# Mixer projections with the high half of the weights meeting both halves of x in one 512-column matmul

## The chip, the cores and the metric

The kernel runs on one core of a Trainium2 chip. The metric is the device time of one launch in microseconds (us). Five engines work beside each other, each through its own queue in order: PE (TensorE, matrix products), ACT (ScalarE), DVE (VectorE), POOL (GpSimd) and SP (which issues transfers). PE writes to PSUM banks; ACT and DVE read them.

## The reference

An encoder trunk of two layers over 256 positions of width 1024, in float32. Each layer adds half a SwiGLU feed-forward block, a mixer, and another half feed-forward block:

```python
for l in range(DEPTH):
    x = x + FFN_RES * swiglu(rms_norm(x, ffn1_norm[l]), ffn1_w_gate[l], ffn1_w_up[l], ffn1_w_down[l])
    h = rms_norm(x, mix_norm[l])
    proj = h @ w_in[l]
    xr, gate, q, k, v = jnp.split(proj, SPLITS, axis=-1)
    y_rec = recurrent_group(xr, gate, conv_w[l], conv_b[l], lru_w_a[l], ...)
    y_att = windowed_gqa(q, k, v, attn_sink[l], rel_bias)
    y = jnp.concatenate([rms_norm(y_rec, lru_out_norm[l]), rms_norm(y_att, attn_out_norm[l])], axis=-1)
    x = x + y @ w_out[l]
    x = x + FFN_RES * swiglu(rms_norm(x, ffn2_norm[l]), ffn2_w_gate[l], ffn2_w_up[l], ffn2_w_down[l])
return rms_norm(x, final_norm)
```

In the mixer, `xr` goes through a convolution of four taps, two gates and a scan in each direction; `gate` goes through a GELU and multiplies the result of the scans; `q`, `k` and `v` feed attention with a window.

## The kernel before

Float32 products are made from split operands: every matrix is held as a high half, rounded to the fast float32 form, and a low half, the rest. A product is three matmuls: high by high, high by low, low by high. x is normed, transposed and split into one tile `xhl` that holds for each of 8 blocks of 128 rows its high half (256 columns, one per position) and its low half beside each other. Weights arrive as float32 (`raw`), are rounded by ACT (line 297; eight mixer halves by DVE, line 295) into `wh`, and DVE subtracts (line 298) to get `wl`. They go through a ring of eight slots and are prepared some pieces ahead of their use.

In the feed-forward stages `proj_pair` (lines 556 to 566) makes a tile of 128 outputs: per block one matmul of `wh` with both halves of x (512 columns) and one of `wl` with the high half (256 columns). The bank then holds two partial results, and `whole` (lines 741 to 746) adds them: ACT copies the second half of the bank to SBUF (line 744), DVE adds the first half to it (line 745).

In the mixer stage, `unit` (lines 827 to 831) makes a tile of 128 outputs with `proj` (lines 547 to 554): per block three matmuls of 256 columns, all into the same 256 columns of a bank, which hold the whole result. `unit` is called 12 times in each of the two layers: four times for the recurrence (`xr`, then `conv`, lines 860 to 876), four for its gate (`gelu`, lines 913 to 919) and four for the queries (`q`, lines 1089 to 1093, which splits the result into `q_t` on ACT and `ql_t` on DVE). All of them read the bank directly.

The order of the mixer's steps on PE is written out in `ORDER` (line 59) and is fixed, as are those of SP and POOL:

```python
ORDER = "x0 k0 x1 q0 l0 q1 l1 L0 x2 L1 x3 g0 l2 P0 q2 l3 V0 P1 s0 L2 g1 c0 c1 q3 V1 P2 L3 c2 y0 g2 y1 V2 P3 g3 c3 V3 D0 y2 y3 r0 O0 r1 O1 r2 r3 R0 R1 R2 R3 S0".split()
```

x, g and q are the three kinds of `unit`. l makes the gates of the recurrence from the convolved tile, c scans, y multiplies with the gate and splits, s takes a square root of all of it on ACT. L makes the logits of two heads from `q_t` and `ql_t`, P transposes the probabilities, V applies them to the values, D norms, O transposes the attention's result, r and R are the output product of the recurrent half. The order of ACT's and DVE's instructions is not written out in this stage: it is chosen when the program is built, by a planner with a cost model of its own. Banks of the pools `ps_c` and `ps_g` are handed out in turn (two of each), for the units, l and L; r and R take both banks of one of these pools.

Of the kernel before, what the change touches and what calls it, by code (L numbers as in the profile page):

```python
# [8 lines left out]
F32 = mybir.dt.float32  # L9
F32R = mybir.dt.float32r  # L10
AF = mybir.ActivationFunctionType
ALU = mybir.AluOpType
# [8 lines left out]
T = 256  # L21
# [46 lines left out]
def encoder_kernel(  # L68
# [31 lines left out]
    pe, act, dve, pool = nc.tensor, nc.scalar, nc.vector, nc.gpsimd  # L100

    def P(name, bufs, **kw):
        return ctx.enter_context(tc.tile_pool(name=name, bufs=bufs, **kw))
# [9 lines left out]
    sum_p = P("sum", 1)  # L113
# [11 lines left out]
    def bank(pool_):  # L125
        if pool_ == "gc":
            turn.append(turn.pop(0))
            pool_ = turn[0]
        return {"a": ps_a, "b": ps_b, "g": ps_g, "c": ps_c}[pool_].tile([128, 512], F32, tag=pool_, name="ps_" + pool_)
# [177 lines left out]
    def prefetch(target):  # L307
        while state["half"] <= min(target, state["cap"], len(halves) - 1):
            j = state["half"]
            n = turns.get(halves[j][0], 0)  # L310
            if n >= SLOTS and ring[n - SLOTS] not in used:
                return
            with ExitStack() as behind:
                for ins in state["behind"]:
                    behind.enter_context(tc.issue_after(ins.ins))
                prep_one()

    def W(*name):
        prefetch(index[name] + state["ahead"])
        return slot_t[name]  # L320

    def done(name):
        used.add(name)
        del slot_t[name]
# [222 lines left out]
    def proj(dst, w, t0, t1):  # L547
        wh, wl = w
        xh, xl = cur["h"], cur["l"]
        for k in range(KD):  # L550
            ks = slice(k * 128, (k + 1) * 128)
            pe.matmul(dst, wh[:, ks], xh[:, k, t0:t1], start=(k == 0), stop=False)  # L552
            pe.matmul(dst, wh[:, ks], xl[:, k, t0:t1], start=False, stop=False)
            pe.matmul(dst, wl[:, ks], xh[:, k, t0:t1], start=False, stop=(k == KD - 1))

    def proj_pair(dst, w):

        wh, wl = w
        x2 = cur["x"]
        for k in range(KD):  # L560
            ks = slice(k * 128, (k + 1) * 128)
            if k:
                pe.matmul(dst[:, 0:T], wl[:, ks], x2[:, 0, k, :], start=False, stop=False)  # L563
            pe.matmul(dst, wh[:, ks], x2[:, :, k, :], start=(k == 0), stop=(k == KD - 1))  # L564
            if not k:
                pe.matmul(dst[:, 0:T], wl[:, ks], x2[:, 0, k, :], start=False, stop=False)
# [248 lines left out]
    def mix(l):  # L815
        st = (l, 1)
# [6 lines left out]
        kl_t = mix_p.tile([128, T], F32R, tag="kl", name="kl_t")  # L823
        kv_t = mix_p.tile([128, 2, 256], F32, tag="kv", name="kv_t")
        late = {}

        def unit(name, i):
            ps = bank("gc")[:, 0:T]
            proj(ps, W(st, name, i), 0, T)
            done((st, name, i))  # L830
            return ps

        def head(t):
            if t == 0:
# [20 lines left out]
        def xr(i):  # L855
            ps = unit("xr", i)
            with tc.high_priority(offset=MIXF):
                conv(i, ps)
# [226 lines left out]
        def body():  # L1085
            def gate(i):
                gelu(i, unit("gt", i))

            def q(i):
                ps = unit("q", i)  # L1090
                act.activation(out=q_t[:, i, :], in_=ps, func=AF.Copy, scale=0.125)
                dve.scalar_tensor_tensor(out=ql_t[:, i, :], in0=ps, scalar=0.125, in1=q_t[:, i, :].bitcast(F32),
                                         op0=ALU.mult, op1=ALU.subtract)

            def den(_):
                att_den()
                att_norm(0)
                att_norm(1)

            def root(_):  # L1100
                act.activation(out=late["w"], in_=late["w"], func=AF.Sqrt)

            def stats(_):
                rec_stats()
                rec_evac(0)

            step = {"x": xr, "g": gate, "q": q, "l": lru_gate, "k": lambda _: head_end(), "s": root, "c": lru_scan,
                    "y": y_rec, "r": lambda k: rec(0, [k]), "R": lambda k: rec(1, [k]), "S": stats,
                    "L": att_logits, "P": att_pt, "V": att_pv, "D": den, "O": o_split, "f": lambda _: turn.reverse()}
            for n, i in ORDER:  # L1110
                step[n](int(i))
                if n == "D":
                    load_gain(3 * l + 2)
# [4 lines left out]
    with tc.manual_schedule(engines={engines.PE, engines.SP, engines.Pool}):  # L1118
        stages = [ffn((0, 0), None)]
        step = {"s": first_squares, "n": first_norm, "T": first_transposes, "m": stages[0][0]()}  # L1120
        for n, f in (("h", first_split), ("w", first_prep)):
            step[n] = lambda *a, f=f: f(False, *a)
            step[n.upper()] = lambda *a, f=f: f(True, *a)
        with tc.manual_schedule(engines={engines.Activation, engines.DVE}):
            setup_early()
            for _ in range(RAWS + 1):
                load_raw()
            for tok in FIRST:
                ins = step[tok[0]](*map(int, tok[1:]))
                if tok in BEHIND:  # L1130
                    state["behind"].append(ins)
        prefetch(3 + LEAD)
        state["behind"] = [ins]
        prefetch(3 + LEAD2)
        state["behind"] = []
        load_gain(1)
        for s in range(3 * DEPTH):
            _, body, tail, evac = stages[s]
            body()
            n = s + 1  # L1140
            if n == 3 * DEPTH:
                with tc.manual_schedule(engines={engines.Activation, engines.DVE}):
                    finish(tail, evac)
                break
            stages.append(mix(n // 3) if n % 3 == 1 else ffn((n // 3, n % 3), None))
            first = index[(n // 3, n % 3), "kv", 0] if n % 3 == 1 else index[(n // 3, n % 3), "g", 0]
            boundary(tail, evac, n, stages[n][0], first + (MAHEAD if n % 3 == 1 else 3))
# [46 lines left out]
```

## Time and profile before

| | |
|---|---|
| three runs | 951.38, 952.01, 953.37 us (median 952.01) |
| the profiled execution's own time | 952.4 us |
| its span | 950.6 us |
| PE busy | 927.3 us, 98% of the span |
| DVE busy | 705.0 us, 74% |
| ACT busy | 540.0 us, 57% |
| mean granted clock of PE | 0.992 of 2.4 GHz |

The span is the time from the first to the last instruction of the profiled execution. A share of busy time is an average over stages; which engine sets the pace in one stage has to be read from that stage. Matmuls are pipelined, so their durations overlap; the distance from one start to the next is what a matmul costs in a row of matmuls. The same is true to a smaller degree of DVE and ACT. Rows of a timeline have start and duration in us, engine, line of the kernel, operation, tile written and tiles read, count, and, in brackets, idle time before and what ended it.

### The profile page before, as it was taken

What the parts mean: (1) busy time and instruction counts of PE and PEld (TensorE: products, weight loads), DVE (VectorE), ACT (ScalarE), POOL (GpSimd) and SP (SyncE); (2) the same over time, 40 slices, a digit from 0 to 9 for tenths busy, and PEclk for the clock granted to TensorE, in tenths of its full rate; (3) what the DMA queues carried; (4) which work ended last, traced back from release to release, by engine and by line L of the source; (5) the groups of instructions that cost most, each with busy time, mean ns of one, the idle gap of its engine ahead of it and who ended that gap; (6) DMA issues with size and microseconds to landing.
All of it is one profiled execution on the core that took longest, in us unless ns stands there. A gap on an engine that the chain in (4) does not pass through costs nothing.

```text
span 950.6 us, 13902 instructions
## 1 busy us (share of the span) xinstructions
PE 927.3 (98%) x5407; PEld 811.6 (85%) x5407; DVE 705.0 (74%) x1192; ACT 540.0 (57%) x986; POOL 56.4 (6%) x66
## 2 busy tenths in 40 slices
PE   6799999999999999999999999999999999999997
PEld 6688888889989888888887888888999898888885
DVE  6967766768998866666589666666799887666663
ACT  7555555647864655555455555555587565555542
POOL 4400000000010000000070000000000100000000
PEclk9899999999999999999999999999999999999998
DMA  8865865625254856555646565556152566566521
GB/s 280 261 212 188 301 208 196 204 85 177 90 155 143 278 183 207 186 180 192 204 131 224 180 207 190 179 189 208 45 193 95 180 201 220 180 197 199 178 89 44
DMA packets 124994, 172.56 MB, mean 182 GB/s; under 512 B 3920, under 2 KB 108792, under 8 KB 124928
## 3 DMA queue, kind: packets, MB, share of 16 engines
q1 hardware_dynamic: 122192, 166.21, 54.3%
q0 software_dynamic: 2288, 4.87, 1.6%
q8 instruction: 42, 0.69, 0.3%
q10 hardware_dynamic: 448, 0.59, 0.2%
q14 instruction: 24, 0.20, 0.1%
HBM read 170.59 MB, written 3.16 MB: 183 GB/s over the span
## 4 chain that ended last, share of the span: by engine, by line
PE 91%; DVE 4%; ACT 2%; DMA 2%; issue 1%; POOL 0%; SPq 0%; POOLq 0%; DVEq 0%; ACTq 0%
PE ps_g L564 15%; PE ps_c L564 15%; PE ps_g L563 7%; PE ps_c L563 7%; PE ps_a L573 4%; PE ps_a L575 4%; PE ps_a L574 4%; PE ps_b L575 4%; PE ps_b L574 4%; PE ps_b L573 4%; PE ps_c L544 2%; PE ps_g L544 2%; DVE wl L298 1%; PE ps_a L997 1%; PE ps_g L552 1%
## 5 line engine op out<-in xcount | busy, mean ns | idle before, releaser
L298 DVE TENSOR_TENSOR wl<-raw,wh 128x1024 fp32r<-128x1024 f32 (+1 forms) x308 | 374.3, 1221 | 106.1 <-ACT wh L297 101.1
L297 ACT ACTIVATE wh<-raw 128x1024 fp32r<-128x1024 f32 (+1 forms) x294 | 300.3, 1032 | 87.3 <-PE ps_b L575 63.4
L564 PE MATMUL ps_g<-xhl,wh 128*128 128x512 f32 x640 | 233.7, 399 | 4.9 <-DVE hl L733 4.9
L564 PE MATMUL ps_c<-xhl,wh 128*128 128x512 f32 x640 | 232.6, 398 | 0.0
L563 PE MATMUL ps_g<-xhl,wl 128*128 128x256 f32 x560 | 157.3, 281 | 0.0
L563 PE MATMUL ps_c<-xhl,wl 128*128 128x256 f32 x560 | 156.7, 280 | 0.0
L564 PEld LDWEIGHTS ps_g<-xhl,wh 128*128 128x128 f32 x640 | 121.2, 189 | 28.5 <-issue 5.2
L564 PEld LDWEIGHTS ps_c<-xhl,wh 128*128 128x128 f32 x640 | 121.0, 189 | 23.1
L563 PEld LDWEIGHTS ps_g<-xhl,wl 128*128 128x128 f32 x560 | 106.6, 190 | 3.5
L563 PEld LDWEIGHTS ps_c<-xhl,wl 128*128 128x128 f32 x560 | 106.3, 190 | 3.5
L573 PE MATMUL ps_a<-wh,hh 128*128 128x512 f32 x168 | 65.8, 391 | 0.0
L573 PE MATMUL ps_b<-wh,hh 128*128 128x512 f32 x168 | 65.6, 391 | 0.0
L575 PE MATMUL ps_b<-wh,hl 128*128 128x512 f32 x168 | 65.4, 389 | 0.0
L575 PE MATMUL ps_a<-wh,hl 128*128 128x512 f32 x168 | 65.4, 389 | 0.0
L574 PE MATMUL ps_b<-wl,hh 128*128 128x512 f32 x168 | 65.4, 389 | 0.0
L574 PE MATMUL ps_a<-wl,hh 128*128 128x512 f32 x168 | 65.4, 389 | 0.0
L744 ACT ACTIVATE sg<-ps_g 128x256 f32<-128x256 f32 x40 | 15.4, 384 | 60.5 <-PE ps_g L564 60.2
L744 ACT ACTIVATE sg<-ps_c 128x256 f32<-128x256 f32 x40 | 15.4, 384 | 58.5 <-PE ps_c L564 58.4
L492 POOL TENSOR_TENSOR rstd<-rstd,half_t 128x1 f32<-128x1 f32 x16 | 11.2, 701 | 616.7 <-DVE rstd L489 488.2
L745 DVE TENSOR_TENSOR sg<-ps_g,sg 128x256 f32<-128x256 f32 x40 | 17.0, 425 | 31.8 <-ACT sg L744 31.8
L744 ACT ACTIVATE su<-ps_c 128x256 f32<-128x256 f32 x40 | 15.5, 386 | 40.8 <-PE ps_c L564 40.8
L744 ACT ACTIVATE su<-ps_g 128x256 f32<-128x256 f32 x40 | 15.4, 385 | 40.4 <-PE ps_g L564 40.4
(316 smaller groups left out, 1685.1 us busy)
## 6 DMA issues: line engine op xcount, KB each, us to landing
raw<-in_ffn_w_down_dram SPq DMA_DIRECT2D x44, 1024.0 KB, 5.0
raw<-in_ffn_w_gate_dram SPq DMA_DIRECT2D x43, 1024.0 KB, 5.4
raw<-in_ffn_w_up_dram SPq DMA_DIRECT2D x43, 1024.0 KB, 5.4
raw<-in_w_in_dram SPq DMA_DIRECT2D x14, 1024.0 KB, 5.4
raw<-in_w_out_dram SPq DMA_DIRECT2D x8, 1024.0 KB, 7.5
lb<-ld POOLq DMA_DIRECT2D x1, 2048.0 KB, 14.9
bias_t<-lb POOLq DMA_DIRECT2D x1, 1536.0 KB, 12.2
gain<-in_ffn_norm_dram SPq DMA_DIRECT2D x3, 512.0 KB, 4.4
```

The costliest lines, as they stand in the source:

```text
L297: act.activation(out=h3, in_=src, func=AF.Copy)
L298: dve.tensor_sub(out=l3, in0=src, in1=h3.bitcast(F32))
L492: pool.tensor_tensor(out=st[:, 1:2], in0=st[:, 0:1], in1=half_t, op=ALU.pow)
L544: pe.matmul(dst, (xh, xh, xl)[p][:, k, ts_], w[k // 4][p % 2][:, c], start=(p == 0 and k == 0), stop=(p == 2 and k == KD - 1))
L552: pe.matmul(dst, wh[:, ks], xh[:, k, t0:t1], start=(k == 0), stop=False)
L563: pe.matmul(dst[:, 0:T], wl[:, ks], x2[:, 0, k, :], start=False, stop=False)
L564: pe.matmul(dst, wh[:, ks], x2[:, :, k, :], start=(k == 0), stop=(k == KD - 1))
L573: pe.matmul(acc[hf], ah[:, ts_], wh[:, cs], start=first, stop=False)
L574: pe.matmul(acc[hf], ah[:, ts_], wl[:, cs], start=False, stop=False)
L575: pe.matmul(acc[hf], al[:, ts_], wh[:, cs], start=False, stop=last)
L744: act.activation(out=s, in_=ps[:, T:2 * T], func=AF.Copy)
L745: dve.tensor_tensor(out=s, in0=ps[:, 0:T], in1=s, op=ALU.add)
```

## The change

`unit` calls `proj_pair` in place of `proj`, takes a tile from the pool `sum_p` (its two buffers, `sg` and `su`, in turn), lets ACT copy the second half of the bank into it and DVE add the first half, and returns this SBUF tile. `conv`, `gelu` and `q` then read SBUF in place of the bank.

```diff
@@ -823,12 +823,17 @@
         late = {}
+        sums = ["sg", "su"]
 
         def unit(name, i):
-            ps = bank("gc")[:, 0:T]
-            proj(ps, W(st, name, i), 0, T)
+            ps = bank("gc")
+            proj_pair(ps, W(st, name, i))
             done((st, name, i))
-            return ps
+            sums.append(sums.pop(0))
+            s = sum_p.tile([128, T], F32, tag=sums[0], name="s")
+            act.activation(out=s, in_=ps[:, T:2 * T], func=AF.Copy)
+            dve.tensor_tensor(out=s, in0=ps[:, 0:T], in1=s, op=ALU.add)
+            return s
```

## Rows read from the trace of the kernel before

**Rows 1.** Page, part 1: busy time, share of the span, instructions of PE.

```profile
PE 927.3 (98%) x5407; PEld 811.6 (85%) x5407; DVE 705.0 (74%) x1192; ACT 540.0 (57%) x986; POOL 56.4 (6%) x66
```

**Rows 2.** Windows: us, busy of PE, PEld, DVE, ACT, POOL (instructions), PEclk, DMA, GB/s.

```profile
213.30:269.60 56.30, 56.24 (x484) 54.79 (x483) 52.25 (x125) 43.70 (x104) 0.00 (x0) 1.00 0.38 125
677.90:734.20 56.30, 56.26 (x484) 54.79 (x483) 52.25 (x125) 43.70 (x104) 0.00 (x0) 1.00 0.38 125
237.00:272.00 35.00, 35.00 (x297) 33.91 (x297) 34.79 (x84) 27.88 (x70) 0.59 (x1) 1.00 0.34 104
```

**Rows 3.** Timeline, PE: the first matmul of unit q0 and what follows the unit.

```profile
219.33 0.28 PE L552 MATMUL ps_c<-xhl,wh 128*128 128x256 f32 x1
...
222.21 0.28 PE L887 MATMUL ps_g<-xch,gh_t 128*128 128x256 f32 x1
```

**Rows 4.** Timeline, PE: two paired units of a feed-forward stage and what follows.

```profile
132.74 0.39 PE L564 MATMUL ps_c<-xhl,wh 128*128 128x512 f32 x1
...
135.56 0.40 PE L564 MATMUL ps_g<-xhl,wh 128*128 128x512 f32 x1
...
138.33 0.39 PE L573 MATMUL ps_a<-wh,hh 128*128 128x512 f32 x1
```

**Rows 5.** Timeline, feed-forward: copy on ACT, add on DVE, its reader, the next.

```profile
138.53 0.39 ACT L744 ACTIVATE su<-ps_g 128x256 f32<-128x256 f32 x1 [1.08 <-PE ps_g L564]
138.81 1.05 ACT L297 ACTIVATE wh<-raw 128x1024 fp32r<-128x1024 f32 x1
130.64 0.42 DVE L745 TENSOR_TENSOR su<-ps_g,su 128x256 f32<-128x256 f32 x1 [0.21 <-ACT su L744]
131.10 0.43 DVE L726 TENSOR_TENSOR th<-th,su 128x256 f32<-128x256 f32 x1
138.95 0.42 DVE L745 TENSOR_TENSOR su<-ps_g,su 128x256 f32<-128x256 f32 x1 [0.21 <-ACT su L744]
```

**Rows 6.** Lines 864 and 406: durations ns (min/median/max), first and last start.

```profile
L864 DVE TENSOR_SCALAR xc<-ps_g,par x6: 540/543/545, 216.4 to 702.1; 128x256 f32<-128x256 f32 x6
L406 DVE TENSOR_SCALAR xn<-x,rstd x8: 347/348/354, 7.0 to 13.7; 128x256 f32<-128x256 f32 x8
```

**Rows 7.** Line 552: what PE sat idle for before it (us, times).

```profile
  DVE xc L867: 0.5, 2
```

**Rows 8.** Timeline, ACT, DVE and PE: from q3 to the logits L3.

```profile
256.82 0.36 ACT L1091 ACTIVATE q_t<-ps_g 128x256 fp32r<-128x256 f32 x1
258.09 0.42 DVE L1092 SCALAR_TENSOR_TENSOR ql_t<-ps_g,q_t 128x256 fp32r<-128x256 f32 x1
258.38 0.28 PE L953 MATMUL ps_c<-kl_t,q_t 64*128 64x256 f32 x1
258.57 0.38 PE L954 MATMUL ps_c<-k_t,ql_t 64*128 64x256 f32 x1
```

**Rows 9.** Timeline, ACT, DVE and PE: from g3 to the product r3.

```profile
268.14 0.38 ACT L916 ACTIVATE x<-ps_g 128x256 f32<-128x256 f32 x1 [0.43 <-PE ps_g L554]
268.17 1.22 DVE L298 TENSOR_TENSOR wl<-raw,wh 128x1024 fp32r<-128x1024 f32 x1
269.31 0.42 DVE L917 SCALAR_TENSOR_TENSOR x<-x,ps_g 128x256 f32<-128x256 f32 x1
271.58 0.69 DVE L295 CAST wh<-raw 128x1024 fp32r<-128x1024 f32 x1
273.09 1.22 DVE L298 TENSOR_TENSOR wl<-raw,wh 128x1024 fp32r<-128x1024 f32 x1
274.22 0.48 DVE L933 SCALAR_TENSOR_TENSOR yl<-i_t,par,yh 128x256 fp32r<-128x256 f32 x1
275.23 0.39 PE L575 MATMUL ps_c<-wh,yl 128*128 128x512 f32 x1
```

**Rows 10.** Timeline, DVE and PE: the end of the mixer stage and the next stage's head.

```profile
286.19 1.21 DVE L298 TENSOR_TENSOR wl<-raw,wh 128x1024 fp32r<-128x1024 f32 x1
293.96 0.28 PE L544 MATMUL ps_c<-wh,xhl 128*128 128x256 f32 x1
```

## Prediction

> **What bounds the kernel now.** I read the page first: PE is busy 98% of the span [rows 1]. So a change pays if it shortens PE's work, as long as PE goes on without waits. The page's share is an average, so I then took the view of windows for the two stretches that the change touches, from the first projection unit of a mixer to the first output product. PE is busy in all but 0.06 us of the 56.3 us, at a granted clock of 1.00, which is the 2.4 GHz level. But DVE is busy for 52.25 us of the same 56.3 us, and ACT for 43.70; the second layer gives the same numbers [rows 2]. Away from the mixer DVE has room (74% over the span, [rows 1]); here it has 4.05 us. Most of this room lies at the start, where DVE has nothing to do until the first unit is done; from 237 to 272 us DVE is busy for 34.79 of 35 us, ACT for 27.88 [rows 2]. So the stage is bound by PE with DVE close behind it, and what has to be asked is whether the change makes DVE, or the chains through ACT and DVE, the bound.
>
> **What PE saves.** Before, a unit is 24 matmuls of 256 columns; q0 takes from 219.33 to 222.21, 2.88 us, which is 0.12 us for each [rows 3]. The paired form is in the trace already, in the feed-forward stages: 16 matmuls, 2.82 us for one and 2.77 us for the next [rows 4]. The saving is 2.88 - 2.82 = 0.06 to 2.88 - 2.77 = 0.11 us per unit; I take 0.08: of 155 such units in the feed-forward timeline 73 last 2.77 or 2.78 and 76 last 2.81 or 2.82. 12 units in a stage give 0.96 us (0.7 to 1.3).
>
> There is a second gain. The bank of a unit is now held until the last of its readers; for the convolution that is DVE's fourth instruction, line 867, and PE waits for it twice, once per layer, for 0.5 us together [rows 7]. After the change the bank is free after the add. So 0.25 us more per stage, if the copy and the add are not late themselves. Together 1.2 us per stage, 2.4 us in all.
>
> [...]
>
> **What ACT and DVE get.** 12 copies and 12 adds per stage. In the feed-forward stages the copy holds ACT for 0.28 us (138.53 to 138.81) and the add follows its start after 0.42 us (138.53 to 138.95); the add's result is used by the next DVE instruction 0.46 us after the add's start (130.64 to 131.10) [rows 5]. So
>
> - ACT has 12 x 0.28 = 3.4 us more, on 43.70 of 56.3.
> - DVE has 12 adds more. The add lasts 0.42 us; with the overlap that ACT shows between neighbours (0.39 us long, 0.28 apart) I count 0.34 of it, as between other neighbours on a busy DVE: 4.1 us. Against this the first step of the convolution, which reads the bank in 0.543 us, will read SBUF; the nearest row for that is the same operation on an SBUF tile, 0.348 us [rows 6]. 4 x 0.195 = 0.8 us less. Net 3.3 us per stage (between 2.5, if other readers gain also, and 5.0, if the adds count in full).
> - Each chain from a unit to its consumer gets 0.42 + 0.46 = 0.88 us longer, if both engines are free at once, and more if the add has to queue.
>
> So DVE's load becomes 52.25 + 3.3 = 55.55 us in a stretch that is to shrink from 56.3 to 55.1. This doesn't fit, unless work leaves the stretch. What can leave it: weight preparation for the tail of the stage. DVE makes two such weights (a rounding, line 295, and a subtraction, line 298; the second at 271.58 and 273.09, the subtraction of the first at 268.17) ahead of the split that r3 needs [rows 9]; each costs 0.6 + 1.2 = 1.8 us, and both are used after r3. Behind r3 DVE's last weight of the stage is done at 287.4, 6.5 us ahead of the next stage's head at 293.96 [rows 10]. So 3.6 us can be put off without harm, if the planner does put them off. No transfer is added or moved; the loads of the next weights start when a raw tile is free, and a preparation put off by 3 us delays them by as much, inside these 6.5 us.
>
> The new copy makes ACT wait for the unit, and for the reader of two units before, since there are two sum buffers. Units are at least 2.9 us apart; behind a copy that waits there stand weight roundings, tanhs and exps, and behind these DVE. I cost this at nothing; if a reader of the convolution is late by more than this distance, it costs what it is late.
>
> **Where PE will wait.** Two places have no room for 0.88 us:
>
> - L3. The split of q3 is late now: ACT comes to it at 256.82, after the exps of the second-last heads, DVE at 258.09 to 258.51, and PE's third logits matmul, normally 0.12 us behind the second, starts 0.19 us behind it, at 258.57 [rows 8]. After the change PE comes to this place earlier by 10 units x 0.08 + 0.25 = 1.05 us, and `ql_t` comes later by up to 0.88 us. So the wait is 1.05 to 1.93 us: everything that was gained so far is lost, whatever its size, and up to 0.88 us more. Least is lost if the copy goes ahead of the exps. I take 1.5.
> - r3. The chain from g3 ends with the split at 274.22 to 274.70, and its matmul starts at 275.23, room of 0.53 us [rows 9]. It gets 0.88 us longer: a wait of 0.35 us. It is 0 if the weight pair goes behind the chain, and about 3 us if the whole load of DVE arrives here. I take 0.25, as the planner had already put these pairs later than others of their kind.
>
> **Sum.** Per stage -1.2 + 1.5 + 0.25 = +0.55 us, for two stages +1.1 us. From the profiled execution (952.4 us, span 950.6) that is 953.5; the median of the runs is 0.4 us lower, so 953.1 us.
>
> **Rivals.**
> 1. All is hidden: the planner places copies and adds well, L3 and r3 don't wait. For it: at most places chains have some 2 us of room, banks come free earlier, and 3.6 us of DVE's work can move. Against it: no room at L3 [rows 8]. 952.0 - 2.4 = 949.6 us.
> 2. DVE becomes the bound, and the time is longer. Mechanism: the planner goes by its own costs and leaves the weight pairs where they are; then 3.3 us of adds and 0.9 us of the first chain's delay, less the 0.53 us of room and some 0.4 of small gaps, end at r3, as PE comes there: 3.3 + 0.9 - 0.53 - 0.4, about +3.3 us per stage against now, less what is put off after all; with one rounding of 0.6 us put off, +2.7. It decides the sign from the point where DVE puts off less than about 2.3 us: then +1.0 per stage is left, over 0.2% in all. For it: DVE's 55.55 in 55.1 us [rows 2]. Against it: the slack behind r3 [rows 10]. 952.0 + 2 x 2.7 = 957.4 us.
> 3. The pairing saves less in the mixer than in the feed-forward stages. At 0.06 us per unit rival 1 gives 952.0 - 1.9 = 950.1; the forecast doesn't move, because there the late split sets the time and not PE. [...]
>
> **Chances.** A difference of 0.2% (1.9 us) is about what a measurement of this kernel can tell from no change. Rival 1 has 0.15 (with rival 3 inside it, some of it within 0.2%), rival 2 has 0.25, the forecast 0.60; its own range is from 951 (L3 waits for only what PE gained) to 955 (both places pay in full, 2 x (0.88 + 0.35 + some queueing)), so a quarter of it is slower by over 0.2%. Faster 0.14, same 0.46, slower 0.40. The range goes from 950.0, which leaves out the lower part of rival 1, to 957.5, which takes in most of rival 2.
>
> **What the profile will show.** Units of 2.77 to 2.82 us with 16 matmuls; line 864 at 0.35 us; no idle time of PE before g0; DVE at over 95% of the stretch; a gap of more than 0.2 us ahead of PE's line 954 in L3, and one ahead of r3; line 295 and 298 pairs behind 274 us. I am wrong if L3 starts a microsecond earlier than now (the copy went ahead), or if DVE's pairs stay and PE waits for 3 us at r3.

## The result and the profile after

The changed kernel takes 964.13 us (median of four runs, 961.04 to 964.44) against 952.27 us of the kernel before on the same chip: a ratio of 1.0118, 95% interval 1.0106 to 1.0130. The forecast was 953.1 us with a range to 957.5. The change costs some 12 us, ten times the 1.1 us that the sum gave.

The page after, part 1, answers [rows 1]:

```profile
PE 931.9 (97%) x5215; PEld 805.3 (84%) x5215; DVE 711.6 (74%) x1216; ACT 547.6 (57%) x1010; POOL 54.3 (6%) x66
```

DVE got 6.6 us more (711.6 against 705.0), ACT 7.6 us (547.6 against 540.0): 3.3 and 3.8 us a stage, where the sum had 3.3 and 3.4. PE has 192 matmuls less, and yet 4.6 us more of busy time. So the work added was sized well, and the loss is elsewhere.

The view of windows for the same two stretches, from the first unit of the mixer of the first layer on, against [rows 2]:

```profile
211.85:268.15 56.30, 52.07 (x337) 45.45 (x335) 50.47 (x125) 43.79 (x106) 0.00 (x0) 0.94 0.35 115
237.00:272.00 35.00, 32.08 (x213) 28.74 (x212) 33.62 (x82) 27.50 (x69) 0.00 (x0) 0.90 0.31 96
```

PE is busy in 52.07 of 56.3 us, where it was in 56.24: 4.2 us of idle time came in. Its clock is 0.94 in place of 1.00. DVE is busier in neither window (50.47 against 52.25 us, 33.62 against 34.79): the stage now gets less far in the same time.

PE's waits, over the whole span (us in total, times, longest), the lines that are new against before:

```profile
PE ps_c L957 <- ACT q_t L1096: 2.9, 2, 1.5
...
PE ps_g L893 <- DVE xcl L881: 2.3, 3, 1.0
PE ps_c L959 <- DVE ql_t L1097: 1.8, 2, 0.9
...
PE ps_c L893 <- DVE xcl L881: 1.0, 2, 0.6
PE ps_g L892 <- ACT xch L880: 0.4, 1, 0.4
```

Lines 957 and 959 are the logits (L3 in the order), lines 892 and 893 the gates of the recurrence (l0 to l2); `xch` and `xcl` are the halves of the convolved tile's split. The waits come to 8.4 us. None of them is at r3: from 262 to 296 us no row of PE shows idle time.

The next table follows PE through both mixer stages: each step's start against the same step before, both counted from the stage's first matmul, as the PE timelines of the two traces have them. The stage grew from 80.60 to 87.32 us, the second from 80.59 to 87.16. Together that is 13.3 us; the first stage begins 1.5 us earlier than before (211.85 against 213.36), in work that the change doesn't touch.

| up to the start of | us later than before, stage 1 | stage 2 | what lies between |
|---|---|---|---|
| l0 | -0.19 | -0.22 | three units, each 0.04 to 0.11 shorter |
| L0 | +1.61 | +0.30 | waits for `xcl` in l0 (stage 1 alone) and l1 |
| g0 | +1.07 | -0.23 | two units; the bank wait of [rows 7] is gone |
| P0 | +1.68 | +1.51 | wait for `xcl` in l2, in stage 2 for `xch` as well |
| P2 | +1.67 | +1.49 | |
| L3 | +3.20 | +3.03 | wait for `q_t` |
| g2 | +4.85 | +4.66 | L3: wait for `ql_t`, then slower matmuls |
| V2 | +6.79 | +6.62 | the unit g2 itself, at half the clock |
| end | +6.72 | +6.57 | nothing more |

So a stage loses some 1.6 us up to P2, after what the units save, and some 5 us between P2 and V2; the sum had 0.55 us in all.

**Around L3.** The timeline of after, on ACT, DVE and PE, against [rows 8]:

```profile
257.25 0.19 ACT L971 ACTIVATION_READ_ACCUMULATOR pr<-pr,stn 128x1 f32 x1
257.34 0.36 ACT L834 ACTIVATE s<-ps_c 128x256 f32<-128x256 f32 x1
257.61 0.36 ACT L834 ACTIVATE s<-ps_g 128x256 f32<-128x256 f32 x1
257.98 1.09 ACT L990 ACTIVATE pt<-ps_b 128x512 f32<-128x512 f32 x2
259.06 0.42 ACT L921 ACTIVATE x<-s 128x256 f32<-128x256 f32 x1
259.39 0.42 ACT L1096 ACTIVATE q_t<-s 128x256 fp32r<-128x256 f32 x1
...
257.69 0.66 DVE L912 SCALAR_TENSOR_TENSOR i_t<-i_t,w_t 128x512 f32<-128x512 f32 x1
258.28 0.41 DVE L932 TENSOR_TENSOR i_t<-i_t 128x256 f32<-128x256 f32 x1
258.61 0.41 DVE L835 TENSOR_TENSOR s<-ps_c,s 128x256 f32<-128x256 f32 x1
258.95 0.41 DVE L835 TENSOR_TENSOR s<-ps_g,s 128x256 f32<-128x256 f32 x1
259.28 0.67 DVE L914 TENSOR_TENSOR_SCAN i_t<-a_t,i_t 128x256 f32<-128x256 f32 x1
259.88 0.66 DVE L916 TENSOR_TENSOR_SCAN i_t<-a_t,i_t 128x256 f32<-128x256 f32 x1
260.46 0.39 DVE L922 SCALAR_TENSOR_TENSOR x<-x,s 128x256 f32<-128x256 f32 x1
260.77 0.41 DVE L1097 SCALAR_TENSOR_TENSOR ql_t<-s,q_t 128x256 fp32r<-128x256 f32 x1
...
259.85 0.38 PE L957 MATMUL ps_c<-k_t,q_t 64*128 64x256 f32 x1 [1.47 <-ACT q_t L1096]
261.24 0.58 PE L959 MATMUL ps_c<-k_t,ql_t 64*128 64x256 f32 x1 [0.89 <-DVE ql_t L1097]
```

Before, the last exp ended at 256.65:

```profile
256.46 0.19 ACT L966 ACTIVATION_READ_ACCUMULATOR pr<-pr,stn 128x1 f32 x1
```

ACT then split q3 straight from the bank, behind one step of the GELU (256.82), and DVE followed at 258.09. Now q3 goes ACT, DVE, ACT, DVE, and it queues at each step. ACT copies it at 257.61; DVE, which has no idle time here, adds it at 258.95, behind a step of the scans (line 912), one of y0 (line 932) and the add of g1; only then can ACT make `q_t` (259.39); DVE makes `ql_t` at 260.77, behind two scans and a step of the GELU. From the last exp's end (257.44 now, 256.65 before) to the logits' third matmul are 3.8 us in place of 1.9: 1.9 us longer, where the working had at most 0.88. The exps themselves end 2.3 us later in the stage than before, 0.6 us more than PE's own delay at P2; the waits at L3 are made of both.

**Behind L3.** Windows of 1 us; the figure behind POOL's bracket is the granted clock:

```profile
258.00:259.00 1.00, 0.38 (x4) 0.15 (x2) 1.00 (x4) 1.00 (x2) 0.00 (x0) 1.00 0.00 0
259.00:260.00 1.00, 0.15 (x1) 0.15 (x2) 1.00 (x4) 0.80 (x3) 0.00 (x0) 1.00 0.00 0
260.00:261.00 1.00, 0.35 (x2) 0.15 (x2) 1.00 (x3) 0.12 (x1) 0.00 (x0) 0.73 0.00 0
261.00:262.00 1.00, 0.76 (x6) 0.76 (x8) 1.00 (x4) 0.30 (x1) 0.00 (x0) 0.50 0.00 0
...
266.00:267.00 1.00, 1.00 (x4) 0.81 (x4) 1.00 (x4) 0.20 (x2) 0.00 (x0) 0.50 0.00 0
267.00:268.00 1.00, 1.00 (x8) 0.93 (x7) 0.20 (x1) 0.06 (x1) 0.00 (x0) 0.85 0.41 90
268.00:269.00 1.00, 1.00 (x11) 1.00 (x11) 0.65 (x2) 1.00 (x3) 0.00 (x0) 1.00 1.06 279
```

PE is idle for most of 258 to 261 us; then its clock is 0.50, the 1.2 GHz level, up to 267. The unit g2 takes from 262.82 to 267.74, 4.92 us, where it took 2.98 before (259.48 to 262.46). The first matmul of g2 and of V2 behind it, before and after:

```profile
259.48 0.39 PE L552 MATMUL ps_c<-xhl,wh 128*128 128x256 f32 x1
262.46 1.90 PE L997 MATMUL ps_a<-kv_t,pt 128*128 128x64 f32 x16
...
262.82 0.79 PE L564 MATMUL ps_c<-xhl,wh 128*128 128x512 f32 x1
267.74 1.89 PE L1002 MATMUL ps_a<-kv_t,pt 128*128 128x64 f32 x16
```

The matmuls of L3, from line 959's first to g2, take 1.58 us (261.24 to 262.82) in place of 0.91 (258.57 to 259.48). So the clock costs 1.94 + 0.67 = 2.6 us a stage, and the waits ahead of it 1.5 + 0.9 = 2.4. The Trainium skill ("TensorE: Matmul & The Clock Gate", section "Part 1: The HAM clock gate") says that an idle TensorE falls back to the lower of two clock levels. The rows agree on the level, 0.50; PE had not been wholly idle before it, but busy for 0.88 of the 3 us.

**At l0.** Timeline of DVE and PE, after:

```profile
219.12 0.69 DVE L295 CAST wh<-raw 128x1024 fp32r<-128x1024 f32 x1 [1.21 <-DMA raw<-in_w_in_dram]
219.85 1.23 DVE L298 TENSOR_TENSOR wl<-raw,wh 128x1024 fp32r<-128x1024 f32 x1
...
220.99 0.42 DVE L881 TENSOR_TENSOR xcl<-xc,xch 128x256 fp32r<-128x256 f32 x1
...
221.46 0.39 PE L893 MATMUL ps_g<-xcl,gh_t 128*128 128x256 f32 x1 [0.67 <-DVE xcl L881]
```

`xch` was ready at 218.36. But DVE had by then gone to a weight whose data hadn't landed, waited 1.21 us for it, and made both halves of it before the split that PE needed. Here DVE is not short of time: the split stands in the wrong place of its queue. In the second stage DVE's order is the same, but the weight had landed (DVE rounds it at 689.07, right behind the convolution), and PE doesn't wait at l0. So the loss at l0 also hangs on when a transfer lands. Before, only the rounding stood ahead of the split, and the subtraction behind it; `xcl` was done at 220.41 and PE read it at 222.33, right behind the start of l0 in [rows 3]:

```profile
219.99 0.42 DVE L876 TENSOR_TENSOR xcl<-xc,xch 128x256 fp32r<-128x256 f32 x1
```

That is 1.9 us of room.

### The profile page after: what moved, and what is told of

It reads as the page before. It is cut to its first block, busy times and chain, and to the rows that moved or that the text cites. A ratio compares the mean times of both kernels' runs of the same rounds, so it can differ in the third digit from the quotient of the medians.

```text
span 962.3 us, 13552 instructions
## 1 busy us (share of the span) xinstructions
PE 931.9 (97%) x5215; PEld 805.3 (84%) x5215; DVE 711.6 (74%) x1216; ACT 547.6 (57%) x1010; POOL 54.3 (6%) x66
## 4 chain that ended last, share of the span: by engine, by line
PE 82%; DVE 10%; DMA 3%; issue 2%; ACT 2%; POOL 0%; POOLq 0%; ACTq 0%; DVEq 0%
PE ps_g L564 16%; PE ps_c L564 16%; PE ps_g L563 7%; PE ps_c L563 7%; PE ps_a L573 4%; PE ps_a L575 4%; PE ps_a L574 4%; PE ps_b L575 4%; PE ps_b L573 4%; PE ps_b L574 4%; DVE wl L298 3%; PE ps_c L544 2%; PE ps_g L544 1%; DMA raw<-in_w_in_dram 1%; PE ps_g L566 1%
## 5 line engine op out<-in xcount | busy, mean ns | idle before, releaser
L564 PE MATMUL ps_g<-xhl,wh 128*128 128x512 f32 x752 | 274.1, 399 | 4.5 <-DVE hl L733 4.5
L564 PE MATMUL ps_c<-xhl,wh 128*128 128x512 f32 x720 | 265.4, 402 | 0.0
L563 PE MATMUL ps_g<-xhl,wl 128*128 128x256 f32 x658 | 184.3, 280 | 0.0
L563 PE MATMUL ps_c<-xhl,wl 128*128 128x256 f32 x630 | 177.7, 282 | 0.0
L564 PEld LDWEIGHTS ps_g<-xhl,wh 128*128 128x128 f32 x752 | 141.9, 189 | 32.0 <-issue 4.8
L564 PEld LDWEIGHTS ps_c<-xhl,wh 128*128 128x128 f32 x720 | 137.7, 191 | 27.2 <-PE ps_g L958 0.4
L563 PEld LDWEIGHTS ps_g<-xhl,wl 128*128 128x128 f32 x658 | 124.8, 190 | 4.1
L563 PEld LDWEIGHTS ps_c<-xhl,wl 128*128 128x128 f32 x630 | 121.3, 192 | 4.1
L492 POOL TENSOR_TENSOR rstd<-rstd,half_t 128x1 f32<-128x1 f32 x16 | 9.2, 577 | 629.6 <-DVE rstd L489 487.4
L732 ACT ACTIVATE hh<-th 128x256 fp32r<-128x256 f32 x80 | 33.4, 417 | 8.5 <-DVE th L726 8.2
```

What stands on the lines that cost most here:

```text
L732: act.activation(out=hh, in_=src, func=AF.Copy)
```

## The experiments

Two theories went into them. "Chains": the copy and the add lengthen the way from a unit to its reader, the reader is late at l0 to l2 and L3, and the clock falls behind L3. "Load": DVE is simply full, and each added operation counts alike, wherever it stands. A third was that paired matmuls are slower here. In every version the planner chose the order on ACT and DVE anew, so a run can differ in other places than the edited one.

### One half of the change alone

e1_pair_only calls `proj_pair` and returns the first half of the bank; e2_sum_only keeps the old matmuls and does the copy and a second pass over the bank:

```diff
 e1, against after:
             proj_pair(ps, W(st, name, i))
             done((st, name, i))
-            sums.append(sums.pop(0))
-            s = sum_p.tile([128, T], F32, tag=sums[0], name="s")
-            act.activation(out=s, in_=ps[:, T:2 * T], func=AF.Copy)
-            dve.tensor_tensor(out=s, in0=ps[:, 0:T], in1=s, op=ALU.add)
-            return s
+            return ps[:, 0:T]
 e2, against before:
             proj(ps, W(st, name, i), 0, T)
             done((st, name, i))
-            return ps
+            sums.append(sums.pop(0))
+            s = sum_p.tile([128, T], F32, tag=sums[0], name="s")
+            act.activation(out=s, in_=ps, func=AF.Copy)
+            dve.tensor_tensor(out=s, in0=ps, in1=s, op=ALU.max)
+            return s
```

> The change's matmuls without its copy and add: conv, gelu and q read the first 256 columns of the bank, so the product of the high half of the weights with the low half of x is left out of the 24 units. Theory 'chains' (the time comes from the copy and the add in the way of l0, l1, l2 and L3): PE keeps its saving, 952.3 - 2.4 = 950 us, from 949 to 951. Rival 'the paired matmuls are slower in the mixer': clearly above 953 us, towards 964. Theory 'load' (DVE is simply full) gives 950 too.

> The three 256-column matmuls of before, with a copy on ACT and an operation of the add's size on DVE behind each unit (a maximum of the bank and its copy, which gives the same values). Theory 'chains': the waits are set by ACT and DVE, not by PE, so nearly the whole loss is here without the change's matmuls: 963 to 966 us. Rival 'paired matmuls': about 952 to 954. Theory 'load': like 'chains'.

Measured: e1 952.7 us, ratio 1.0008 [0.9999, 1.0018]; e2 961.69 us, ratio 1.0095 [1.0074, 1.0117]. The loss is in the copy and the add: e2 alone has four fifths of it, with the waits at the same places, though less than the 963 us and more that were expected. That paired matmuls are slower is out: e1 has them and none of the loss. That e1 isn't faster was a miss. Its units are shorter by 0.07 us each, as costed, but the stages are 80.63 and 81.24 us long against 80.60 and 80.59. PE's waits in e1 show where that went:

```profile
PE ps_c L564 <- DVE xc L868: 1.6, 2, 1.2
PE ps_g L564 <- ACT i_t L897: 0.4, 2, 0.2
```

PE arrives earlier at banks that the convolution (line 868) or the gates' reader (line 897) still hold, and waits there. In this order of the steps PE's gain was not to be had, even without the copy and the add; e12 below has it in another order.

### One kind of unit at a time

Each of these uses the new form for one name only, and the old form for the others (`if name not in (...)` ahead of the new lines):

> The change for the four query units of each layer alone; the others as before. Theory 'chains': the wait at L3 (3.2 us per stage in the trace of the changed kernel) and the fall of the clock behind it (1.9) are both here, the waits at l0, l1, l2 (0.8 to 0.9 each) are not: 2 x 5.1 less 8 x 0.08, 961 to 962 us. Theory 'load' (each added operation counts alike, a third of 12 us): 956 us.

> The change for the four recurrence units of each layer alone. Theory 'chains': the waits at l0, l1 and l2 for the split of the convolved tile are here (0.8 to 0.9 us each per stage in the changed kernel), the wait at L3 isn't: 2 x (2.6 less 0.35 of bank wait and 0.3 of matmuls), 956 us. Theory 'load': a third of 12 us, 956 us too; the stretches of the trace tell them apart: under 'chains' PE's loss stands at l0 to l2, nothing at L3.

> The change for the four gate units of each layer alone: the same number of added operations as for q or x, but their result is needed late (y), so no tight chain gets longer. Theory 'chains': 952 us, between 951 and 953.5. Theory 'load': a third of 12 us like each other kind, 956 us.

Measured: queries 959.68 us, ratio 1.0076 [1.0054, 1.0099]; recurrence 956.68, 1.0041 [1.0023, 1.0059]; gate 954.06, 1.0024 [1.0015, 1.0034]. Four copies and four adds a stage cost 2 us or 7, depending on who reads the result. The queries' figure lies between the two theories (956 and 961 to 962). With the queries alone there are the waits at L3 and the clock's fall (the unit g2 +2.06 and +1.15 us in the two stages). With the recurrence alone the expected cost was at l0 to l2; it turned out to be smaller there (0.7 us between l0 and L0, of which 0.1 is left at P0) and larger at L3 (+1.35), where DVE made `ql_t` 0.7 us late and the GELU of g1 held the bank of g2 for 0.5 us; in the second stage the clock fell behind it (g2 +1.51 us). So the delay turns up at another place than the lengthened chain, and the pure "chains" reading was too narrow. With the gate alone the small loss is spread over L3 and the end of the stage, between both expectations (952 and 956).

### The clock behind L3

e4_fill keeps the change and gives PE twelve matmuls of 512 columns, whose results no one reads, ahead of L3:

```diff
+            if i == 3:
+                for n in range(12):
+                    pe.matmul(banks[n % 2], cur["h"][:, n % KD, 0:128], cur["x"][:, :, n % KD, :], start=True, stop=True)
```

> The changed kernel with 12 matmuls of 512 columns more per layer (2.8 us at 2.4 GHz) ahead of the logits L3, into banks that L3 then overwrites. If the fall of the clock to 1.2 GHz behind L3 comes from PE's wait there, PE now works through the 1.5 us and most of the 0.9 us in which it waited, keeps 2.4 GHz, and g2 takes 2.9 us in place of 4.9: 964 less 2 x 2 us or some more, 959 to 961 us, although PE has 5.6 us more to do. If the clock falls for another reason, the time is the same or longer: 964 to 967 us.

Measured: 958.17 us, ratio 1.0062 [1.0047, 1.0077], a little under the 959 to 961 us expected. With some 5.5 us more of PE work (24 matmuls 0.23 us apart), the kernel is some 6 us shorter than after. Two windows of it:

```profile
260.00:261.00 1.00, 1.00 (x13) 0.97 (x12) 1.00 (x4) 0.28 (x1) 0.00 (x0) 1.00 0.00 0
261.00:262.00 1.00, 1.00 (x7) 0.79 (x6) 1.00 (x3) 0.51 (x1) 0.00 (x0) 1.00 0.00 0
```

The clock stays at 1.00, and g2 is 0.09 us shorter than before in the first stage, in place of 1.94 longer. From P2 to V2 the stage is 2.4 us longer than before, some 2.7 us of it the fillers, where after is 5.1 us longer: the fillers fill the waits, and the 2.7 us a stage that are won are about the clock's fall. The waits at l0 to l2 are smaller too (+0.50 and +0.40 at P0, where after has +1.68 and +1.51), so some 2.3 us of the gain come from there. This shows the clock's part of the loss; as the fillers cover the waits as well, it doesn't size it to the tenth.

### More room for the chains

e7_l3_later puts g2 ahead of L3, g3 ahead of P3 and r0 ahead of V3; e9_both_later also q1 ahead of l0, x2 ahead of l1, and so on. e10 and e11 are the kernel before with the same orders, e12 is e1 with both shifts:

```diff
 e7:
-... q3 V1 P2 L3 c2 y0 g2 y1 V2 P3 g3 c3 V3 D0 y2 y3 r0 O0 ...
+... q3 V1 P2 g2 L3 c2 y0 y1 V2 g3 P3 c3 r0 V3 D0 y2 y3 r1 O0 ...
 e9, besides:
-x0 k0 x1 q0 l0 q1 l1 L0 x2 L1 x3 ...
+x0 k0 x1 q0 q1 l0 x2 l1 L0 x3 L1 ...
```

> The changed kernel with the unit g2 ahead of L3 in the order of PE's steps (and g3 ahead of P3, r0 ahead of V3, so that the steps behind L3 have cover as well); the same work. Theory 'chains': the split of q3 has 2.8 us more, the wait at L3 (3.2 us) and the low clock behind it (1.9) go, while l0 to l2 still wait: 964 - 10 and up to 1 us of new waits per stage, 954 to 956 us. Theory 'load': DVE's work is the same, so PE waits elsewhere: 962 us or more.

> The changed kernel with two shifts in the order of PE: L3 one or two steps later as in e7 (there 4.1 us over before were left), and now also l0 behind q1 in place of ahead of it, l1 behind x2, L0 and L1 one step later each. Chains: what e7 had left is mostly the waits ahead of l0, l1 and l2; they go too, 953 to 955 us. Load: VectorE has as much to do, and the waits turn up at other steps behind it; no change against e7, 956 to 957 us.

> The kernel before with only the shift of e7 in its order (L3, P3 and V3 later). A control: if the shift itself costs something (a wait ahead of O0, where e7 had 1.2 us), it is 953 to 955; if the shift is free, 951.5 to 952.5; both theories say at least 951.

> The kernel before with both shifts of e9. A control, as e10: 951 to 953 if the shifts are free; 953 to 955 if the later l tiles make the scans late.

> Paired matmuls alone, without copy and add (so the product of the low half of the weights' partner, weights high by x low, is left out of the result), with both shifts of e9. If PE's saving of 0.07 us a unit was eaten by handoffs at L3, l0 and g0 only because they had no room, more room lets it show: 950 to 951 us. If ACT and DVE set the pace of the whole stage, nothing is gained by more room either: 952 to 953.

| | us | ratio to before |
|---|---|---|
| e7_l3_later | 956.11 | 1.0046 [1.0029, 1.0062] |
| e9_both_later | 954.84 | 1.0037 [1.0022, 1.0052] |
| e10_before_l3_later | 951.42 | 0.9994 [0.9985, 1.0004] |
| e11_before_both | 954.03 | 1.0015 [1.0005, 1.0025] |
| e12_pair_both | 952.99 | 1.0007 [0.9998, 1.0017] |

The one shift of e7 takes some 60% of the loss away, the waits at L3 and the clock's fall; in the kernel before it is free (e10). Part of it, 1.3 us, stands ahead of P0 in the first stage, where PE doesn't wait at l0 this time. With both shifts the waits at l0 to l2 are gone as well, and at P1 PE is 0.68 us ahead of before: there the forecast gain of the units stands. It is lost again behind that, e9:

```profile
PE ps_b L1032 <- DVE o L1016: 2.4, 2, 1.2
...
PE ps_c L957 <- ACT q_t L1096: 1.7, 2, 0.8
...
PE ps_c L959 <- DVE ql_t L1097: 0.5, 2, 0.3
```

`q_t` and `ql_t` are late at L2 now, and `o`, the attention's normed result, at O0. So 2.7 us stay against the kernel before. But this order isn't free: e11, the kernel before with both shifts, is 0.15% slower than before, clear of noise, with a wait of its own for a bank:

```profile
PE ps_c L952 <- DVE xc L867: 1.2, 2, 0.6
```

Order against order, the stages of e9 take 82.42 and 82.44 us and those of e11 81.89 in both: there the change costs 0.5 us a stage. e12, the pairing alone, equals the kernel before, which was to mean that ACT and DVE set the pace. But against e11 its stages are 0.83 us shorter (81.06 in both), which is what 12 units save, and its median is 1.0 us lower. So with more room the saving of the pairing does show; the order that gives the room costs more than that, 1.3 us a stage (81.89 against 80.60).

### Priority

e8_prio has the change's order, but lets the planner rank copy and add above other work:

```diff
-            act.activation(out=s, in_=ps[:, T:2 * T], func=AF.Copy)
-            dve.tensor_tensor(out=s, in0=ps[:, 0:T], in1=s, op=ALU.add)
+            with tc.high_priority(offset=400):
+                act.activation(out=s, in_=ps[:, T:2 * T], func=AF.Copy)
+                dve.tensor_tensor(out=s, in0=ps[:, 0:T], in1=s, op=ALU.add)
```

> The changed kernel with a higher priority for the added copies and adds, so that the planner puts them ahead of other ready work: on ACT the copy of q3 behind the first of the four exps and no longer behind the fourth. Theory 'chains': the split of q3 is ready about 1.2 us earlier, the wait at L3 is about 2 us in place of 3.2, and if the clock stays up 1.9 us more are won: 958 to 962 us. Theory 'load': no change, 964 us.

Measured: 959.23 us, ratio 1.0070 [1.0052, 1.0088]. The wait for `q_t` and the clock's fall behind L3 are gone in both stages; `ql_t`, which has no such rank, still comes 0.9 us late, and PE is late at P2 and P3 (the exps' results, five waits of up to 0.3 us). In the second stage the clock falls at another place, to 0.5 from 709.0 to 712.5, behind waits of 0.9 and 0.7 us for `xch` and `xcl` in l2. The place in the queues decides some 5 us with the work unchanged.

### Less work for DVE

If the loss is DVE's load, it must shrink with it. Of the seven weight roundings that DVE makes in a stage (line 295, 14 in both stages of before), one (e13, VG = 0) or four (e14 to e16, VO = 3 as well) were moved to ACT, in the changed kernel (e13, e16), in e9 (e14) and in e10 (e15):

```diff
-VO = 6
-VG = 1
+VO = 3
+VG = 0
```

> The changed kernel, with one weight rounding a stage (that of the first gate piece, VG = 0) on ScalarE in place of VectorE. In the changed kernel this rounding and its subtraction stand ahead of the split xcl, on which l0 waits; behind it l1 and l2 wait too. Chains: the 1.4 to 2.4 us a stage that PE loses ahead of P0 shrink by a half or more, and 960 to 962 us in all. Load: 0.6 us of VectorE a stage goes, so some 1.2 us in all, and the waits ahead of l0, l1, l2 stay: 962 to 963.

> The kernel with both shifts of the order (e9, 2.7 us over before), with four weight roundings a stage (VO = 3, VG = 0) on ScalarE in place of VectorE: 2.4 us of VectorE's work less a stage, 4 us of ScalarE's more. If what e9 has left is VectorE's load, its waits ahead of L2, g1 and O0 go and it comes to 951 to 952.5. If it is the longer chains, which go through ScalarE as well, it stays at 954 to 956 or grows.

> The kernel before with the shift of e10 and the same four roundings on ScalarE. A control: VectorE wasn't the bound there, so nothing is gained, 951 to 952.5 us; more if ScalarE becomes late with its exps and copies.

> The changed kernel in its own order, with the same four roundings on ScalarE. VectorE's load a stage is then 3.3 - 2.4 = 0.9 us over that of before. Load: the loss falls to a third, 955 to 956.5 us. Chains: the waits at L3 come from what is queued ahead of the copy and the add there; they shrink by what the queue gets shorter and no more, and the clock still falls behind them, 958 to 962.

| | us | ratio to before |
|---|---|---|
| e13_after_one_cast | 959.01 | 1.0071 [1.0056, 1.0086] |
| e14_both_dve_less | 959.75 | 1.0079 [1.0064, 1.0094] |
| e15_before_dve_less | 955.28 | 1.0034 [1.0022, 1.0046] |
| e16_after_dve_less | 966.73 | 1.0146 [1.0129, 1.0163] |

DVE's busy time doesn't set the loss: by the page e16 has only 2.5 us of DVE over before (707.5 against 705.0), and it is the slowest kernel of all, above what either theory expected; e14 loses 4.9 us against e9. As the roundings went to ACT, these runs alone don't clear DVE. But e7 and e8 leave both engines' work as it is, and some 60% and 40% of the loss go. In e16 and e14 the lateness has moved to ACT's side. PE's waits in e16:

```profile
PE ps_c L957 <- ACT q_t L1096: 4.9, 2, 2.5
...
PE ps_g L892 <- ACT xch L880: 1.6, 2, 0.8
PE ps_c L892 <- ACT xch L880: 1.4, 2, 0.7
PE ps_g L893 <- DVE xcl L881: 1.3, 2, 0.6
```

`q_t` is 2.5 us late, `ql_t` only 0.2. And neither engine is full. The window of e16 over the same first 56.3 us of the stage:

```profile
213.56:269.86 56.30, 51.61 (x331) 44.94 (x330) 48.87 (x123) 46.41 (x109) 0.00 (x0) 0.94 0.33 113
```

DVE has 7 us free in it and ACT 10, and still their results are late. That is as one would expect where the pieces of a chain lie on both engines in turn and what stands ahead of each counts; no run takes it apart further. In e14 much of the loss is the clock again: it falls behind L2 (waits of 1.15 and 0.90 us in the first stage), and g1 takes 5.22 and 4.45 us, where it took 2.98. e15 shows ACT's side on the kernel before: 4 us of rounding a stage put on ACT cost 3.3 us in all there. e13 was expected at 960 to 962; it gains more, for another reason than the one named: the wait at l0 is gone, but `xch` on ACT is 0.7 to 0.8 us late at the following l, and P0 comes later than in after (+2.24 and +2.30). What it gains is at L3, where the waits are 1.0 us and 0.4 us, and the clock no longer falls (g2 -0.06 us).

What stays open is how much of the 2.7 us of e9 is DVE's load, ACT's load or the order of the steps: e14 changed the first two and the planner's order with them. No version beat the kernel before; e10 equals it.

## Why the prediction was wrong, point by point

- **PE bound with DVE close behind.** Right as read from the windows, but it didn't follow that PE's saving becomes time, nor did the forecast's other half, that PE loses only where a chain is already late. e1 shows the banks as tight as PE in this order: 1.7 us of saving in 24 units gave nothing. With more room, e12 against e11, the saving is there.
- **A unit saves 0.08 us.** Right: the units with no wait beside them were shorter by 0.04 to 0.11, e1's by some 0.07. The bank wait of [rows 7] went too (g0 comes 0.3 us nearer in the first stage).
- **Line 864 at 0.35 us.** Wrong, without weight. Line 869, the same operation on SBUF (ns, min/median/max):

```profile
L869 DVE TENSOR_SCALAR xc<-s,par x8: 404/408/415, 215.9 to 710.4; 128x256 f32<-128x256 f32 x8
```

The row it was taken from wasn't quite the same operation: line 406 multiplies by one value per partition, line 869 multiplies by one and adds another. Whether that makes the difference isn't shown.

- **ACT 3.4, DVE 3.3 us more a stage.** Right: 3.8 and 3.3.
- **Chains to l0 to l2 at nothing.** The first step that failed. The text gave most places "some 2 us of room", with no row for it, and the sum has no term for l0 to l2. It is 1.9 us of waits in the first stage and 1.8 in the second (with the shifts of e9 none). At l0 the room was there, 1.9 us, and more than the 0.88 us of copy and add; but it was taken up in DVE's queue, where the split now stands behind a weight's rounding and subtraction, and in the first stage behind that weight's landing. Why the planner put the subtraction first isn't shown.
- **L3, taken at 1.5 us.** The place was right, the size wrong. Of the bounds 1.05 to 1.93 the first part was PE coming earlier; PE came 1.67 us later, and the chain was later still, by 2.4 us of waits, where the sum had 1.5. The working priced one copy and one add at 0.88 us; two more crossings between engines also each meant a place in a queue without idle time. e3 shows the mechanism by itself.
- **No term for the clock.** The text took 1.00 from [rows 2] for granted. Behind the 2.4 us of waits it went to 0.50, and that added 2.6 us a stage, more than the waits. e4 and e7, without these waits, have no such fall. The trace of before had the sign: in a feed-forward stage PE waits 2.5 us for DVE, and behind that its clock is 0.50:

```profile
500.62 0.97 PE L718 MATMUL ps_g<-eye_t,th 128*128 128x128 f32 x4 [2.51 <-DVE th L725]
...
502.00:504.00 2.00, 2.00 (x8) 1.71 (x7) 2.00 (x5) 1.34 (x2) 0.00 (x0) 0.50 0.96 321
```

- **r3, and rival 2.** Rival 2 named DVE and the slower side, but at r3, from DVE's total against the stretch. There was no wait there: behind L3, with PE that late, DVE has idle time (busy for 0.20 of the us from 267, 0.65 of the next). The runs on load (e13 to e16), with e7 and e8, show that a total is the wrong measure in any case. The slower side had a chance of 0.40, and the range ended 6.6 us short of the time.

## What to carry to other kernels

Price an inserted step not by its duration alone, but by the number of times that its result crosses between engines, and for each crossing by what stands ahead of it in that engine's queue at that moment; a total of busy time didn't tell here. Where PE, at full clock, is made to wait, count with a fall of its clock behind the wait as a possible cost: here it cost 2.6 us behind 2.4 us of waits, and behind like waits in other runs nothing. And before a saving on the busiest engine is counted, try the saving by itself; where banks are tight, as here, the order as it stands may not let it through. A run with a changed order is read against the old kernel in that same order, as e12 shows.

## What the runs showed of the hardware

The clock's fall was not tied to the wait alone. In e2 the two stages have like waits at L3 (1.4 and 0.8 us); in the first g2 was 1.99 us longer, in the second the clock stayed at 1.00 (windows of e2, second stage):

```profile
732.00:733.00 1.00, 0.26 (x2) 0.27 (x2) 1.00 (x3) 0.68 (x3) 0.00 (x0) 1.00 0.00 0
733.00:734.00 1.00, 0.24 (x2) 0.03 (x1) 1.00 (x4) 0.31 (x1) 0.00 (x0) 1.00 0.00 0
734.00:735.00 1.00, 0.95 (x11) 0.81 (x11) 1.00 (x4) 0.11 (x2) 0.00 (x0) 1.00 0.00 0
```

e5 shows it closer still: in both stages PE waits 0.68 us for `ql_t` and 0.52 us for the bank of g2; in the first stage g2 then takes 2.98 us, as before, in the second 4.47. And the wait of 2.5 us ahead of line 718, behind which the clock fell in the trace of before, is there in e9 and e11 as well, where the clock is 1.00 from 495 to 515 us. So like waits can differ by 2 us of what follows; what decides between them stays open. Three of the four runs of the changed kernel took 964.1 to 964.4 us at a mean clock of 0.988, one 961.04 at 0.991; a fall less in that one would fit, but it has no trace of its own.
